# Stick-breaking scan over pairs of columns, with the diagonal cut by a mask matmul

## Chip, core and metric

The kernel runs on one core of one Trainium2 chip. The metric is the time of one execution on the device in microseconds (us), lower is better; a time given for a kernel is the median of several runs.

## What is computed

One decoder layer over 1024 tokens of width 1024, in float32: an input projection, two attention groups side by side (stick-breaking attention with 8 heads of 64, and latent attention with 4 heads), an output projection, and an MLP. The change touches only the stick-breaking group, per head:

```
z = q_blk @ k_pre.T * SB_SCALE
strict = s_idx < t_idx
sp = where(strict, softplus(z), 0)
excl = cumsum(sp, reverse=True) - sp
a = where(strict, exp(log_sigmoid(z) - excl), 0)
out = a @ v_pre
```

Since exp(-softplus(z)) is sigmoid(-z), the weight of column s is sigmoid(z_s) times the product of sigmoid(-z) over the later columns that lie below the diagonal. The kernel computes this product with a running multiplication from the last column to the first.

## The kernel before

The stages of the program are: input projection of the latent columns and of v, then the stick-breaking stage (with the projection of q and k, and later of the latent queries and keys, filled in between its steps), then latent attention, the output projection, and the MLP, whose products take more than half of the time.

The stick-breaking stage has 96 steps. A step is one block of 128 queries of one head (`j` of 0 to 3 in a half `Q` of the sequence) against up to 512 keys (half `C`). Where `C == Q` the block lies on the diagonal and has n = 128, 256, 384 or 512 columns for j = 0 to 3; there are 16 such groups of four. The other 8 groups of four have n = 512 and carry on a product from the diagonal group before them. Of the 96 steps 48 have n = 512.

A step passes over the engines as follows. TensorE (PE) makes the scores `z` with two matmuls. ScalarE (ACT) makes `w = sigmoid(-z)` (L531) and `b = sigmoid(z)` (L532). VectorE (DVE) runs the scan in place over `w`, backwards (L536). The scan's second operand is a slice of `zid`, zeros with an identity at its end: on the diagonal it starts the product at 1 at each row's own diagonal column, and what lies right of it stays 0. The factor `b` is then multiplied by the scan's result, shifted by one column (L542). This multiplication is on GpSimd (POOL) for odd `j`, and for `j` = 2 too in the last three heads; else on DVE. Where a later group needs the product so far, ACT copies one column of `w` into `carry` (L539). Six steps later PE transposes `b` (L549), ACT and DVE split the transposed block into a high part `ah` and a low part `al` (L556, L557), and PE multiplies with v.

PE's instructions stand in the order in which the program is written (a manual schedule). Those of the other engines are put in order by the compiler's scheduler and run in that order, each behind its waits. `w` has three buffers, `b` ten. The first instruction on a new `w` is a memset of its last column on POOL (L529).

The bfloat16 identity `identb` and the mask `mask_incl` for the latent attention are made late, when that stage is prepared; the same kind of mask matmul that the change brings stands at L746 in the latent attention.

Of the kernel before, what the change touches and what calls it, by code (L numbers as in the profile page):

```python
# [9 lines left out]
F32 = mybir.dt.float32  # L10
F32R = mybir.dt.float32r
BF16 = mybir.dt.bfloat16
I32 = mybir.dt.int32
AF = mybir.ActivationFunctionType
ALU = mybir.AluOpType
# [4 lines left out]
NEG = -1e30  # L20
# [3 lines left out]
def tile_hymba_block(  # L24
# [17 lines left out]
    nc = tc.nc  # L42
    P = 128
# [3 lines left out]
    SBH, SBD = 8, 64  # L47
# [13 lines left out]
    const = ctx.enter_context(tc.tile_pool(name="const", bufs=1, reuse_waits="tile"))  # L61
# [2 lines left out]
        nc.vector.memset(f(z_[:, :, 0:P]), 0.0)  # L64
    mhalf = const.tile([P, 16], F32, name="mhalf")
    nc.gpsimd.memset(mhalf[:], -0.5)
    zid = const.tile([P, 4 * P + 1], F32, name="zid")
    nc.gpsimd.memset(zid[:], 0.0)
    identf = zid[:, 3 * P:4 * P]
    make_identity(nc, identf)  # L70
    ones1 = const.tile([P, 1], F32, name="ones1")
    nc.gpsimd.memset(ones1[:], 1.0)
    gc = const.tile([P, gcols.shape[1]], F32, name="gc")
# [442 lines left out]
    sb_a, sb_carry, sb_t, sb_av = {}, {}, {}, {}  # L516

    def sb_z(h, Q, C, j):
        qs, kh, kl = stacks[h]
        diag = C == Q  # L520
        t = 4 * Q + j
        n = (j + 1) * P if diag else 512
        nn = max(n, 256)
        z = z_ps.tile([P, 512], F32, name="z", tag="z")
        ks = slice(C * 512, C * 512 + nn)
        nc.tensor.matmul(z[:, :nn], qs[:, t * P:(t + 1) * P], kh[:, ks], start=True, stop=False)
        nc.tensor.matmul(z[:, :nn], qs[:, t * P:(t + 1) * P], kl[:, ks], start=False, stop=True)
        w = sw_pool.tile([P, 513], F32, name="w", tag="w", bufs=3)
        nc.gpsimd.memset(w[:, n:n + 1], 1.0)  # L529
        b = sw_pool.tile([P, 512], F32, name="b", tag="b", bufs=10)  # L530
        nc.scalar.activation(w[:, :n], z[:, :n], AF.Sigmoid, scale=-SB_SCALE)  # L531
        last_sig[0] = nc.scalar.activation(b[:, :n], z[:, :n], AF.Sigmoid, scale=SB_SCALE)  # L532
        init = 0.0 if diag else sb_carry[h, j][:]
        rv = w[:, :n + 1][:, ::-1]
        inject = zid[:, 4 * P - n:][:, ::-1] if diag else zid[:, 0:1].to_broadcast([P, n + 1])
        nc.vector.tensor_tensor_scan(rv, rv, inject, init, ALU.mult, ALU.add)  # L536
        if C > 0:
            carry = sw_pool.tile([P, 1], F32, name="carry", tag="carry", bufs=4)
            nc.scalar.copy(carry[:], w[:, 0:1])  # L539
            sb_carry[h, j] = carry  # L540
        eng = nc.gpsimd if (j % 2 or (h >= SBH - 3 and j)) else nc.vector
        eng.tensor_mul(b[:, :n], b[:, :n], w[:, 1:n + 1])  # L542
        sb_a[h, Q, C, j] = b

    def sb_tr(h, Q, C, s):
# [52 lines left out]
    def sb_step(n):  # L598
        h = n // 12 + 1
        if n % 12 == 6 and h % 2 and h < SBH - 1:  # L600
            stack_head(h)
        if n == 3 * NS // 4:
            stack_head(SBH - 1, 0)
        if 0 <= n - LAG < NS:
            sb_tr(*idx[n - LAG])
        if n < NS:
            sb_z(*idx[n])
# [5 lines left out]
    fill = in_proj_pair(0)  # L613
# [9 lines left out]
    def in_proj_rest():  # L623
        for p in range(1, NPAIR):
            yield from in_proj_pair(p)
# [18 lines left out]
    fill = in_proj_rest()  # L644
# [35 lines left out]
    def l8(shape, dt=F32R):  # L680
        return lat_pool.tile(shape, dt, name="l8", tag="l8", bufs=5)

    p0_pool = lat.enter_context(tc.tile_pool(name="p0_pool", bufs=1, side="right", reuse_waits="tile"))
    identb = p0_pool.tile([P, P], BF16, name="identb")
    make_identity(nc, identb)
    mask_incl = p0_pool.tile([P, P], BF16, name="mask_incl")
    nc.gpsimd.memset(mask_incl[:], 0.0)
    nc.gpsimd.affine_select(mask_incl[:], mask_incl[:], pattern=[[-1, P]],
                            compare_op=ALU.is_ge, fill=NEG, base=0, channel_multiplier=1)
# [74 lines left out]
    def lat_gen():  # L764
        for h in range(3):
            yield from mla_qk(h, lambda: lat_ps[0]())

    LAT_START = n0 + 3
    fill = lat_gen()
# [151 lines left out]
    s01, n = iter(range(4)), 0  # L921
# [13 lines left out]
    for n in range(n, NTA * (MH - 1)):  # L935
        h, i = divmod(n, NTA)
# [3 lines left out]
        elif 0 < h < MH - 1 and i % 3 < 2:  # L940
            j = i // 3 * 2 + i % 3
# [558 lines left out]
```

## Time and profile before

| | us |
|---|---|
| median of 3 runs | 1235.33 (1234.29 to 1235.84) |
| the profiled execution | 1236.29 |
| its span, first to last instruction | 1234.5 |
| stick-breaking stage in it, first scan to the last steps | 148 to 365, 217 long |
| DVE busy in that stage | 205.5 |
| PE busy in that stage | 180.2 |
| ACT and POOL busy in that stage | 144.3 and 113.7 |

The span is part of the profiled execution's own time; 1.8 us lie around it. Busy time of an engine is the time in which at least one of its instructions ran. An instruction that is held up by another engine after it has started counts as busy, so a duration that is longer than that of its twins is read as a wait.

### The profile page before, as it was taken

The numbers are of one execution on the slowest core, as the hardware profiler recorded it, in microseconds if no ns is written. First come the engines' busy times: TensorE is split into PE (matmuls) and PEld (weight loads), VectorE is DVE, ScalarE is ACT, GpSimd is POOL, SyncE is SP. The second block draws the span as 40 slices with busy tenths as digits, with TensorE's granted clock in tenths as the row PEclk, the third lists the DMA queues.
The fourth block names the chain that finished last, engine by engine and source line by source line (L and its number), as shares of the span: only waits on it lengthen the run. The fifth ranks groups of instructions, "written<-read, shape, count | busy, mean of one in ns | idle before, by whom it ended". The sixth has DMA issues, their size and how long they took to land. (4 is left out here: it accounts for less than half of the span.)

```text
span 1234.5 us, 15926 instructions
## 1 busy us (share of the span) xinstructions
PE 1155.6 (94%) x5424; PEld 941.7 (76%) x5424; DVE 958.0 (78%) x1310; ACT 535.5 (43%) x1080; POOL 647.2 (52%) x539
## 2 busy tenths in 40 slices
PE   9998988888779999999789999999999999999996
PEld 8886866666658888888567788888777888888885
DVE  8686499999997874553979967666498899888995
ACT  6334456667766772245422222222223333333344
POOL 3343454445653353132755655556447766667667
PEclk9999999999999999999889999999999999999998
DMA  6424833332622225475336544443578435454313
GB/s 214 120 68 156 220 82 78 91 91 59 184 107 90 69 69 188 154 255 168 107 130 208 203 151 159 156 154 128 190 248 300 161 119 170 169 171 143 113 52 137
DMA packets 101586, 179.87 MB, mean 146 GB/s; under 512 B 9216, under 2 KB 53760, under 8 KB 100736
## 3 DMA queue, kind: packets, MB, share of 16 engines
q1 hardware_dynamic: 101504, 178.84, 45.0%
q8 instruction: 43, 0.70, 0.2%
q14 instruction: 39, 0.32, 0.1%
HBM read 111.70 MB, written 54.53 MB: 135 GB/s over the span
## 5 line engine op out<-in xcount | busy, mean ns | idle before, releaser
L1437 PE MATMUL dn<-s,s 128*128 128x512 f32 x1344 | 308.6, 392 | 4.4 <-DVE s L1075 2.3
L1437 PEld LDWEIGHTS dn<-s,s 128*128 128x128 f32 x1344 | 254.4, 189 | 58.4 <-DVE s L1075 2.7
L1075 POOL TENSOR_TENSOR s<-ar,s 128x1024 fp32r<-128x1024 f32 x56 | 147.8, 2641 | 80.8 <-ACT s L1074 80.8
L1075 POOL TENSOR_TENSOR s<-s,s 128x512 fp32r<-128x512 f32 x84 | 117.0, 1414 | 109.8 <-ACT s L1074 109.8
L1441 DVE TENSOR_TENSOR acc<-acc,dn 128x512 f32<-128x512 f32 x224 | 144.0, 678 | 33.8 <-PE dn L1437 32.8
L1074 ACT CAST s<-wr 128x1024 fp32r<-128x1024 f32 x48 | 50.4, 1051 | 150.1 <-PE dn L1437 105.3
L1081 PE MATMUL pa<-b,s 128*128 128x512 f32 x384 | 97.2, 407 | 9.0 <-ACT s L1074 3.7
L1081 PEld LDWEIGHTS pa<-b,s 128*128 128x128 f32 x384 | 74.5, 196 | 27.8 <-ACT s L1074 4.6
L1074 ACT CAST s<-s 128x512 fp32r<-128x512 f32 x84 | 48.3, 620 | 103.3 <-DVE s L1199 59.1
L542 POOL TENSOR_TENSOR b<-b,w 128x512 f32<-128x512 f32 (+2 forms) x57 | 59.5, 1044 | 58.9 <-DVE w L536 39.5
L488 PE MATMUL mm<-xh,wt 128*128 128x512 f32 x256 | 87.9, 396 | 0.0
L549 PE MATMUL tr<-zid,b 128*128 128x128 f32 x288 | 52.8, 290 | 36.4 <-DVE al L557 27.3
L549 PEld LDWEIGHTS tr<-zid,b 128*128 128x128 f32 x288 | 32.9, 142 | 60.2 <-DVE al L557 45.2
L1075 POOL TENSOR_TENSOR s<-wr,s 128x1024 fp32r<-128x1024 f32 x24 | 57.8, 2409 | 32.8 <-ACT s L1074 32.8
L263 PE MATMUL acc<-wt,xh 128*128 128x448 f32 (+1 forms) x256 | 64.8, 389 | 0.9 <-ACT xh L214 0.9
L536 DVE TENSOR_TENSOR_SCAN w<-w,zid 128x129 f32<-128x129 f32 (+1 forms) x64 | 63.9, 1001 | 1.0 <-ACT w L531 0.8
L1074 ACT CAST s<-ar 128x1024 fp32r<-128x1024 f32 x56 | 58.6, 1047 | 9.2 <-DMA ar<-hv_dram 9.2
L1075 DVE TENSOR_TENSOR s<-wr,s 128x1024 fp32r<-128x1024 f32 x24 | 52.4, 2182 | 6.8 <-ACT s L1074 6.8
L263 PEld LDWEIGHTS acc<-wt,xh 128*128 128x128 f32 x256 | 49.5, 194 | 8.9 <-ACT xh L214 1.4
L1081 PE MATMUL pb<-t,s 128*128 128x512 f32 x192 | 49.2, 406 | 6.8 <-ACT s L1074 6.7
L488 PEld LDWEIGHTS mm<-xh,wt 128*128 128x128 f32 x256 | 48.1, 189 | 8.3 <-issue 0.2
L1112 DVE SCALAR_TENSOR_TENSOR ho<-ho 128x512 f32<-128x512 f32 x48 | 51.7, 1076 | 1.4
(335 smaller groups left out, 2688.7 us busy)
## 6 DMA issues: line engine op xcount, KB each, us to landing
ar<-hv_dram SPq DMA_DIRECT2D x56, 512.0 KB, 3.6
s<-in_w_up_dram SPq DMA_DIRECT2D x32, 512.0 KB, 4.6
hv_dram<-s SPq DMA_DIRECT2D x64, 256.0 KB, 2.1
wr<-in_w_down_dram SPq DMA_DIRECT2D x16, 1024.0 KB, 6.9
hv_dram<-ho SPq DMA_DIRECT2D x48, 256.0 KB, 2.1
wr<-in_w_in_dram SPq DMA_DIRECT2D x24, 256.0 KB, 2.9
raw<-in_w_o_dram SPq DMA_DIRECT2D x8, 512.0 KB, 3.6
ht<-h_dram SPq DMA_DIRECT2D x8, 512.0 KB, 4.3
```

The source lines that it names most:

```text
L263: nc.tensor.matmul(accs[t][:, :width], a[:, kk, t * P:(t + 1) * P], wts[kk][:, b, :width], start=(kk == 0 and p == 0), stop=done)
L488: nc.tensor.matmul(ps[:], wt[:, a, k % 4, :], b[:, k, tsl], start=(n == 0), stop=(n == 3 * ND - 1))
L536: nc.vector.tensor_tensor_scan(rv, rv, inject, init, ALU.mult, ALU.add)
L542: eng.tensor_mul(b[:, :n], b[:, :n], w[:, 1:n + 1])
L549: nc.tensor.transpose(tr[:, j * P:(j + 1) * P], sb_a[h, Q, C, j][:, s * P:(s + 1) * P], identf[:])
L1074: nc.scalar.copy(hi, src)
L1075: eng.tensor_sub(lo, src, f(hi))
L1081: nc.tensor.matmul(ps, w[:, a, k, :], bv[:, b, k, :], start=start and n == 0, stop=n == last, skip_group_check=True)
L1112: nc.vector.scalar_tensor_tensor(dst, src, 0.0, src, ALU.max, ALU.mult)
L1437: nc.tensor.matmul(ps[:], av[:, a, u, q * P:(q + 1) * P], bv[i][:, b, u], start=i in (1, 2, 7) and n == 0, stop=n == 5, skip_group_check=True)
L1441: read = nc.vector.tensor_add(dst, dst, ps[:])
```

## The change

For each step, neighbouring columns are first multiplied in pairs (even column times odd column, written to the even column of `w`, on DVE), the scan then runs over the n/2 pair products and one last column, and the final multiplication brings each pair's running product to both columns of the pair. What the even column needs beyond that, the factor of its odd neighbour, is multiplied into the even columns of `b` on POOL. So two instructions of n/2 columns with a step of two are added to each step. The diagonal is cut by a third matmul on the scores (bfloat16 identity times a mask with -1e30 on and above the diagonal), so the scan starts with 1 everywhere and its second operand is one zero column, repeated. `carry` is copied by the engine of the final multiplication instead of ACT. That engine is now POOL for odd `j` and DVE for even `j` in all heads. The bfloat16 identity and the new mask are made at the program's start.

```diff
-    zid = const.tile([P, 4 * P + 1], F32, name="zid")
+    zid = const.tile([P, P + 1], F32, name="zid")
     nc.gpsimd.memset(zid[:], 0.0)
-    identf = zid[:, 3 * P:4 * P]
+    identf = zid[:, 0:P]
     make_identity(nc, identf)
+    zero1 = zid[:, P:P + 1]
+    identb = const.tile([P, P], BF16, name="identb")
+    nc.vector.tensor_copy(identb[:], identf)
+    mask_strict = const.tile([P, P], BF16, name="mask_strict")
+    nc.gpsimd.memset(mask_strict[:], 0.0)
+    nc.gpsimd.affine_select(mask_strict[:], mask_strict[:], pattern=[[-1, P]],
+                            compare_op=ALU.is_gt, fill=NEG, base=0, channel_multiplier=1)
...
-        nc.tensor.matmul(z[:, :nn], qs[:, t * P:(t + 1) * P], kl[:, ks], start=False, stop=True)
+        nc.tensor.matmul(z[:, :nn], qs[:, t * P:(t + 1) * P], kl[:, ks], start=False, stop=not diag)
+        if diag:
+            nc.tensor.matmul(z[:, n - P:n], identb[:], mask_strict[:], start=False, stop=True)
...
-        init = 0.0 if diag else sb_carry[h, j][:]
-        rv = w[:, :n + 1][:, ::-1]
-        inject = zid[:, 4 * P - n:][:, ::-1] if diag else zid[:, 0:1].to_broadcast([P, n + 1])
-        nc.vector.tensor_tensor_scan(rv, rv, inject, init, ALU.mult, ALU.add)
+        init = 1.0 if diag else sb_carry[h, j][:]
+        even, odd = w[:, 0:n:2], w[:, 1:n:2]
+        nc.vector.tensor_mul(even, even, odd)
+        nc.gpsimd.tensor_mul(b[:, 0:n:2], b[:, 0:n:2], odd)
+        rv = w[:, 0:n + 1:2][:, ::-1]
+        nc.vector.tensor_tensor_scan(rv, rv, zero1.to_broadcast([P, n // 2 + 1]), init, ALU.mult, ALU.add)
+        eng = nc.gpsimd if j % 2 else nc.vector
         if C > 0:
             carry = sw_pool.tile([P, 1], F32, name="carry", tag="carry", bufs=4)
-            nc.scalar.copy(carry[:], w[:, 0:1])
+            eng.tensor_copy(carry[:], w[:, 0:1])
             sb_carry[h, j] = carry
-        eng = nc.gpsimd if (j % 2 or (h >= SBH - 3 and j)) else nc.vector
-        eng.tensor_mul(b[:, :n], b[:, :n], w[:, 1:n + 1])
+        b2 = b[:, :n].rearrange("p (k a) -> p k a", a=2)
+        eng.tensor_mul(b2, b2, w[:, 2:n + 1:2].unsqueeze(2).to_broadcast([P, n // 2, 2]))
```

How the instructions stand is shown for the start of one diagonal group in the middle of the stage. The first two pieces are DVE's. A scan has the name SCALAR_TENSOR_TENSOR here and TENSOR_TENSOR_SCAN in the profile; L536 is the scan, L542 the final multiplication, L557 the split of a transposed block. DVE before, a group's four steps (j = 0 to 3):

```order
L536 SCALAR_TENSOR_TENSOR w<-w,zid 128x129
L542 TENSOR_TENSOR b<-b,w 128x128
L152 TENSOR_TENSOR zpad_59<-tr,zpad_59 128x128
L473 CAST wt<-wr 128x512
L536 SCALAR_TENSOR_TENSOR w<-w,zid 128x257
L557 TENSOR_TENSOR al<-tr,ah 128x512
L536 SCALAR_TENSOR_TENSOR w<-w,zid 128x385
L542 TENSOR_TENSOR b<-b,w 128x384
```

DVE of the change at the same place, where L544 is the multiplication of neighbours, L547 the scan, L554 the final multiplication, L569 the split and L480 the cast:

```order
L544 TENSOR_TENSOR w<-w 128x64
L159 TENSOR_TENSOR zpad_59<-tr,zpad_59 128x128
L547 SCALAR_TENSOR_TENSOR w<-w,zid 128x65
L544 TENSOR_TENSOR w<-w 128x128
L554 TENSOR_TENSOR b<-b,w 128x128
L547 SCALAR_TENSOR_TENSOR w<-w,zid 128x129
L480 CAST wt<-wr 128x512
L569 TENSOR_TENSOR al<-tr,ah 128x512
L544 TENSOR_TENSOR w<-w 128x192
L547 SCALAR_TENSOR_TENSOR w<-w,zid 128x193
L554 TENSOR_TENSOR b<-b,w 128x384
```

Each scan now has a multiplication ahead of it, often directly, that writes what the scan reads. Over the stage 28 scans were followed directly by the multiplication that reads their result; now 84 DVE instructions (60 scans, 13 final multiplications, 11 copies of `carry`) stand directly behind the one whose result they read.

The second place is POOL's queue there. POOL before, from the final multiplication (L542) of the last step of the group ahead; L529 is the memset of `w`'s last column (L474 and L495 are the low parts of a weight block and of a projected block):

```order
L542 TENSOR_TENSOR b<-b,w 128x512
L529 MEMSET w 128x1 x2
L542 TENSOR_TENSOR b<-b,w 128x256
L529 MEMSET w 128x1
L474 TENSOR_TENSOR wt<-wr,wt 128x512
L495 TENSOR_TENSOR klo<-y,khi 128x512
```

POOL of the change at the same place, where L545 is the multiplication of the even columns of `b`, L554 the final multiplication, L538 the memset, and L481 and L502 the low parts:

```order
L554 TENSOR_TENSOR b<-b,w 128x512
L545 TENSOR_TENSOR b<-b,w 128x64
L538 MEMSET w 128x1 x2
L545 TENSOR_TENSOR b<-b,w 128x128
L554 TENSOR_TENSOR b<-b,w 128x256
L538 MEMSET w 128x1
L481 TENSOR_TENSOR wt<-wr,wt 128x512
L502 TENSOR_TENSOR klo<-y,khi 128x512
L545 TENSOR_TENSOR b<-b,w 128x192
```

POOL has one more multiplication in every step. The one for j = 2 (128x192) stands behind two 128x512 subtractions, and DVE's final multiplication for j = 2 (L554, 128x384) reads its result.

## Rows read from the trace of the kernel before

**Rows 1.** Page, busy time of the engines, share of the span, instructions.

```profile
PE 1155.6 (94%) x5424; PEld 941.7 (76%) x5424; DVE 958.0 (78%) x1310; ACT 535.5 (43%) x1080; POOL 647.2 (52%) x539
```

**Rows 2.** Stage 148 to 365 us: all instructions, those of L536, those of L542.

```profile
148.00:365.00 217.00, 180.17 (x926) 138.97 (x924) 205.54 (x269) 144.28 (x360) 113.66 (x184) 0.99 0.39 101
...
148.00:365.00 217.00, 112.71 (x96) 0.99 0.39 101
...
148.00:365.00 217.00, 30.61 (x39) 59.23 (x57) 0.99 0.39 101
```

**Rows 3.** Waits in the stage: who waited for whom, us, times, longest.

```profile
POOL b L542 <- DVE w L536: 39.5, 30, 1.7
...
ACT carry L539 <- DVE w L536: 32.4, 29, 3.5
...
PE tr L549 <- DVE al L557: 26.1, 34, 2.2
...
DVE al L557 <- ACT ah L556: 4.9, 9, 0.7
```

**Rows 4.** Timeline of DVE and POOL: start us, us, engine, line, instruction.

```profile
240.85 1.28 POOL L474 TENSOR_TENSOR wt<-wr,wt 128x512 fp32r<-128x512 f32 x1
...
241.24 1.44 DVE L536 TENSOR_TENSOR_SCAN w<-w,zid 128x257 f32<-128x257 f32 x1
...
242.09 1.68 POOL L495 TENSOR_TENSOR klo<-y,khi 128x512 fp32r<-128x512 f32 x1
...
249.22 1.41 POOL L587 TENSOR_TENSOR ssq_s<-ssq_s,avt 64x512 f32<-64x512 f32 x1 [0.76 <-ACT avt L586]
...
249.66 1.53 DVE L542 TENSOR_TENSOR b<-b,w 128x512 f32<-128x512 f32 x1
```

**Rows 5.** Timeline of DVE at moments without a longer twin's delay.

```profile
319.74 0.44 DVE L536 TENSOR_TENSOR_SCAN w<-w,zid 128x129 f32<-128x129 f32 x1
320.28 0.29 DVE L542 TENSOR_TENSOR b<-b,w 128x128 f32<-128x128 f32 x1
320.49 0.68 DVE L557 TENSOR_TENSOR al<-tr,ah 128x512 fp32r<-128x512 f32 x1
...
329.92 0.68 DVE L536 TENSOR_TENSOR_SCAN w<-w,zid 128x257 f32<-128x257 f32 x1
...
331.95 0.95 DVE L536 TENSOR_TENSOR_SCAN w<-w,zid 128x385 f32<-128x385 f32 x1
...
236.87 1.21 DVE L536 TENSOR_TENSOR_SCAN w<-w,zid 128x513 f32<-128x513 f32 x1
...
216.02 0.56 DVE L542 TENSOR_TENSOR b<-b,w 128x384 f32<-128x384 f32 x1
...
227.20 0.69 DVE L542 TENSOR_TENSOR b<-b,w 128x512 f32<-128x512 f32 x1
```

**Rows 6.** Single lines over the whole trace: minimum/median/maximum ns, shapes.

```profile
L536 DVE TENSOR_TENSOR_SCAN w<-w,zid x64: 395/1002/2008, 148.0 to 352.8; 128x129 f32<-128x129 f32 x16, 128x257 f32<-128x257 f32 x16, 128x385 f32<-128x385 f32 x16, 128x513 f32<-128x513 f32 x16
L536 DVE TENSOR_TENSOR_SCAN w<-w,carry,zid x32: 1270/1286/2328, 161.8 to 362.7; 128x513 f32<-128x513 f32 x32
...
L542 POOL TENSOR_TENSOR b<-b,w x57: 637/1093/2012, 150.9 to 364.2; 128x512 f32<-128x512 f32 x35, 128x256 f32<-128x256 f32 x16, 128x384 f32<-128x384 f32 x6
L542 DVE TENSOR_TENSOR b<-b,w x39: 273/692/1533, 148.5 to 357.5; 128x128 f32<-128x128 f32 x16, 128x512 f32<-128x512 f32 x13, 128x384 f32<-128x384 f32 x10
...
L557 DVE TENSOR_TENSOR al<-tr,ah x80: 404/658/694, 156.3 to 371.2; 128x512 fp32r<-128x512 f32 x48, 128x384 fp32r<-128x384 f32 x16, 128x256 fp32r<-128x256 f32 x16
...
L529 POOL MEMSET w<- x96: 93/99/265, 131.6 to 358.3; 128x1 f32 x96
...
L746 PEld LDWEIGHTS <-identb x32: 95/96/98, 363.9 to 462.3; 128*128 128x128 bf16 x32
L746 PE MATMUL s<-mask_incl,identb x29: 229/230/232, 375.6 to 462.3; 128*128 128x128 bf16 x29
```

**Rows 7.** Groups by line and shape, DVE: busy us, mean ns.

```profile
L757 DVE RECIPROCAL mst<-mst 128x1 f32<-128x1 f32 x32 | 5.1, 159 | 8.7 <-ACT pt L756 8.5
```

More of the change, by code (lines that the diff above doesn't have):

```diff
@@ L683, in tile_hymba_block @@
     p0_pool = lat.enter_context(tc.tile_pool(name="p0_pool", bufs=1, side="right", reuse_waits="tile"))
-    identb = p0_pool.tile([P, P], BF16, name="identb")
-    make_identity(nc, identb)
     mask_incl = p0_pool.tile([P, P], BF16, name="mask_incl")
```

## The prediction, made before the changed kernel was run

> **What bounds the kernel now.** The page gives PE 94% of the span and DVE 78% [rows 1], which would make a change on DVE worth nothing. That average hides the stage. The scans run from 148 to 365 us, and there DVE is busy 205.5 of 217 us, PE 180.2, ACT 144.3, POOL 113.7 [rows 2]. DVE is idle for 11.5 us, PE for 37, and the waits say what PE lacks: the largest share of its matmul waits there ends with DVE's low part `al` [rows 3]. DVE in turn waits little for anyone (4.9 us for ACT's `ah`). POOL (39.5 us) and ACT (32.4 us, at the copy of `carry`) wait for DVE's scan [rows 3]. So DVE sets the length of this stage, and outside it the change does next to nothing.
>
> The second thing to see is in DVE's durations. The same scan of 257 columns takes 0.68 us at one time and 1.44 at another [rows 4, 5]. The long one began at 241.24 while POOL's subtraction ran until 242.13, and ended 0.55 later, at 242.68; POOL's next one, begun at 242.09, took 1.68 and ended 1.09 after the scan. The multiplication of 512 columns that takes 0.69 alone began at 249.66, sat out POOL's 1.41 until 250.63, and ended at 251.19 [rows 4, 5]. A DVE instruction with both inputs in SBUF and a POOL one that reads SBUF thus run one after the other. The low part `al`, whose first input lies in PSUM, has a maximum of 0.694 for 512 columns, so it is not held up [rows 6]. Part of DVE's 205.5 us is therefore waiting for POOL.
>
> How much: the 48 shorter-than-512 scans and the 16 diagonal ones of 513 take 16 x (0.44 + 0.68 + 0.95 + 1.21) = 52.5 alone, the 32 with a carry 32 x 1.286 = 41.2 [rows 5, 6], together 93.6; they were busy 112.7 [rows 2], 19.1 more. DVE's 39 final multiplications take 16 x 0.29 + 10 x 0.56 + 13 x 0.69 = 19.2 alone and were busy 30.6, 11.4 more [rows 2, 5, 6]. That is 30.5 us over 135 instructions, 0.23 us each.
>
> **The change on DVE's own work.** Scans: (1.21 - 0.44) / 384 = 2.0 ns per column [rows 5]. With 65, 129, 193 and 257 columns they take 0.31, 0.44, 0.57 and 0.68 alone, with a carry 0.07 more (1.286 against 1.21). New sum 16 x 2.00 + 32 x 0.75 = 56.0, so 37.6 are saved. Added are 96 multiplications of neighbours, n/2 columns each. At the rate of the final multiplication, (0.69 - 0.29) / 384 = 1.04 ns per column [rows 5], they take 0.22, 0.29, 0.36 and 0.42: 16 x 1.29 + 32 x 0.42 = 34.0. Nine final multiplications come over from POOL (6 x 0.56 + 3 x 0.69 = 5.4), and 16 copies of `carry` from ACT; the nearest DVE row of one column is 0.16 [rows 7], 2.6 in all. Sum: -37.6 + 34.0 + 5.4 + 2.6 = **+4.4**.
>
> Instructions also overlap or gap. One that doesn't need its neighbour starts 0.08 before that ends (0.29 from 320.28, next at 320.49); one that reads what its neighbour wrote starts 0.10 after (0.44 from 319.74, next at 320.28) [rows 5]. The order has 28 such direct pairs before and 84 after: 56 x 0.18 = +10.1. The 122 additional instructions give back 122 x 0.08 = 9.8. So +0.3, and DVE's own work grows by about **5 us**: halving the scan buys nothing, since the pair products cost what it saves.
>
> **The unknown stride.** No row shows a DVE instruction that steps over every second float. Below, the step is free. Above, it costs as much as the slowest rate per column here, the scan's 2.0 ns: 0.96 more on 16 x (64 + 128 + 192) + 48 x 256 = 18,432 columns, +17.8, and on the final multiplication's 16 x (128 + 384 + 512) = 16,384, +15.8. The scan takes 2 ns per column already and I give it nothing. I take free: the multiplication by a contiguous neighbour is the nearest row in kind, and two of every four floats that lie together are still read.
>
> [...]
>
> **Waiting for POOL.** POOL gains 96 multiplications. Its own take 0.637 at 256 and 1.093 at 512 columns [rows 6], so 1.8 ns per column and 0.30, 0.41, 0.52, 0.64 for 64 to 256: 16 x 1.87 + 32 x 0.64 = 50.4. Its final ones shrink from 35 x 1.09 + 16 x 0.64 + 6 x 0.87 (between the two) = 53.6 to 32 x 1.09 + 16 x 0.64 = 45.1. The rest of its reading work is 113.7 - 59.2 - 96 x 0.1 = 44.9 [rows 2, 6]. So POOL's time with a read goes from 98.5 to 140.4, by 1.43. DVE's exposed instructions go from 135 to 96 + 96 + 48 = 240. If the wait follows POOL's time it becomes 30.5 x 1.43 = 43.6 (+13); if each instruction still waits 0.23, it is 54.2 (+24). Both are possible, since the added POOL pieces are short; I take the middle, **+18**.
>
> **Other waits.** DVE's final multiplication for j = 0 and 2 now needs POOL's product on `b`, which stands behind POOL's other work, in the piece shown behind two subtractions of 1.3 us. POOL has 140 + 10 us of work in some 240, so it usually gets there; with a full subtraction's wait at the 18 or so places where low parts are made this could reach +23. Against that ACT no longer stands at `carry` for 32.4 us, so `ah` comes sooner, at most the 4.9 us that DVE waits for it [rows 3]. I take **+3**.
>
> PE gains 64 mask matmuls of 0.23 and weight loads of 0.10 [rows 6]. At most 15 us, and its 37 idle us hide them; were the stage bound by PE they would all count. ACT loses 32 copies. Making the mask early is work of under a microsecond on POOL, done while the first loads are under way.
>
> **Sum.** 5 + 18 + 3 = 26 us on the profiled execution's 1236.3 gives 1262. The median of the runs shown is 1.0 below that execution, so **1261 us**, the stage 243 instead of 217.
>
> **Rivals.**
> - The step costs on DVE. Then 17.8 for the pair products, or 33.6 with the final multiplication, come on top: 1279 to 1295. POOL would also be held up longer. Nothing in the trace speaks for or against it.
> - POOL's queue becomes the limit, because its product of two floats per repeated factor runs slower than the contiguous one, or because DVE waits for the even products at each low part: up to +23 - 3, so 1281. For it: two reads in every POOL step that were none. Against it: 150 us of work in a stage of 243 leave POOL time to catch up.
> - Faster: the waits at the SBUF input shrink instead of growing. Scans of half the length hold it for half as long, POOL gets through between them, and its shorter pieces hold DVE for less. With 5 us of own work more and 3 of other waits, the balance is at 30.5 - 8 = 22.5 us over 240 instructions, 0.09 us each in place of 0.23. At 0.04 (10 us) the stage would take 204 and the kernel 1223. Against it: POOL's reading time grows by 42 us in a stage in which DVE already fills 95%.
> - No change: ACT's freed queue and half of that effect just pay for the rest, 1235.
>
> **Chances and range.** Forecast (1245 to 1275) 0.50; stride 0.20; POOL's queue 0.13; faster 0.12; no change 0.05. Slower by over 0.2%, about what a measurement of this kernel can tell from no change: 0.83; within it 0.05; faster 0.12. The range leaves out the faster case and part of no change, and the far end of the stride: 1240 to 1297. The forecast's own range is 1245 to 1275.
>
> **What would show it.** In the stage: scans of 257 columns at 0.68 to 0.75 alone (right on the scan), pair products of 256 at 0.42 (free step) or nearer 0.7 (it costs), pairs directly behind each other 0.10 apart. The sum of excess on DVE's exposed instructions near 48 us (right on the input), under 22 (the faster rival), over 60 (worse). DVE busy over 90% of a longer stage, with PE idle for more than 37 us. Wrong would be a DVE with long idle times that end with POOL's `b`, or a stage in which PE is busy throughout. Outside 148 to 400 us all should stand as before, moved by a constant.

## The result and the profile after

The changed kernel took 1262.95 us (median of four runs, 1261.25 to 1263.32) against 1235.45 for the kernel before on the same chip: a ratio of 1.0221, with a 95% interval of 1.0204 to 1.0239. It is slower by 27.5 us. The forecast was 1261, in a range of 1240 to 1297.

The loss lies in the stick-breaking stage. Its first scan still starts at 147 to 148 us, its last ends at 390.5 instead of 364.0, and what stands before and after has only moved. The page's first part, which answers to [rows 1], shows little of it:

```profile
PE 1165.2 (92%) x5488; PEld 947.5 (75%) x5488; DVE 987.1 (78%) x1432; ACT 534.9 (42%) x1048; POOL 701.1 (56%) x642
```

The windows of the stage answer to [rows 2]. The columns are the window and its length, busy time and instructions of PE, PE's weight loads, DVE, ACT and POOL, the granted clock (as a share of full speed), the DMA share and GB/s. The first row is everything. Then come the scan (L547, DVE alone), the final multiplication (L554, DVE then POOL), the pair product (L544, DVE) and the product on `b` (L545, POOL).

```profile
147.00:391.00 244.00, 191.34 (x992) 144.73 (x990) 235.65 (x390) 144.26 (x328) 166.64 (x285) 0.97 0.35 90
...
147.00:391.00 244.00, 79.11 (x96) 0.97 0.35 90
...
147.00:391.00 244.00, 36.98 (x48) 44.44 (x48) 0.97 0.35 90
...
147.00:391.00 244.00, 60.62 (x96) 0.97 0.35 90
...
147.00:391.00 244.00, 71.98 (x96) 0.97 0.35 90
```

DVE's scans went from 112.7 to 79.1 us, waits included, and the new pair products took 60.6. DVE is busy for 235.7 of 244 us, 30.1 more than before, and idle for 8.3 (before 11.5). PE is idle for 53. POOL went from 113.7 to 166.6 us.

How much of DVE's time is work and how much is being held up is read by setting instructions that nothing held up beside longer ones of the same shape. The timeline of DVE and POOL in the changed kernel (start, duration, engine, line, instruction; in brackets the idle time ahead and what ended it) has both kinds:

```profile
207.90 0.34 DVE L547 TENSOR_TENSOR_SCAN w<-w,zid 128x65 f32<-128x65 f32 x1
208.35 0.29 DVE L554 TENSOR_TENSOR b<-b,w 128x128 f32<-128x128 f32 x1
...
208.76 0.28 DVE L544 TENSOR_TENSOR w<-w 128x128 f32<-128x128 f32 x1
209.07 0.64 DVE L547 TENSOR_TENSOR_SCAN w<-w,zid 128x129 f32<-128x129 f32 x1
...
229.91 0.42 DVE L544 TENSOR_TENSOR w<-w 128x256 f32<-128x256 f32 x1
...
230.85 0.75 DVE L547 TENSOR_TENSOR_SCAN w<-w,carry,zid 128x257 f32<-128x257 f32 x1
...
246.35 0.86 POOL L545 TENSOR_TENSOR b<-b,w 128x256 f32<-128x256 f32 x1
...
246.75 0.74 DVE L544 TENSOR_TENSOR w<-w 128x256 f32<-128x256 f32 x1
...
248.37 1.09 POOL L554 TENSOR_TENSOR b<-b,w 128x512 f32<-128x512 f32 x1 [1.15 <-DVE w L547]
```

The pair product of 256 columns takes 0.42 us alone (229.91). The one at 246.75 began while POOL's product on `b` ran until 247.21, and ended at 247.49, 0.28 later. The new POOL instruction thus holds up the new DVE instruction, in the way that [rows 4] showed for the old ones. This holds for the whole stage: of its 240 scans, pair products and final multiplications on DVE, 121 ran more than 0.08 us over the shortest durations of their shape, and each of the 121 began while a POOL instruction that reads SBUF was running. For 62 of them, with 24 of the 63 us of excess, it was the new product; for 31, with 16 us, a final multiplication. Ninety began with no such instruction running, and none of them was that long; of the other 29, 25 began in the last 0.2 us of one. The whole trace gives minimum, median and maximum ns of each line:

```profile
L547 DVE TENSOR_TENSOR_SCAN w<-w,carry,zid x32: 735/758/1764, 164.6 to 389.8; 128x257 f32<-128x257 f32 x32
...
L544 DVE TENSOR_TENSOR w<-w x96: 193/550/1500, 147.4 to 388.6; 128x256 f32<-128x256 f32 x48, 128x64 f32<-128x64 f32 x16, 128x128 f32<-128x128 f32 x16, 128x192 f32<-128x192 f32 x16
...
L545 POOL TENSOR_TENSOR b<-b,w x96: 343/842/1231, 146.8 to 386.0; 128x256 f32<-128x256 f32 x48, 128x64 f32<-128x64 f32 x16, 128x128 f32<-128x128 f32 x16, 128x192 f32<-128x192 f32 x16
```

The waits of the stage, which answer to [rows 3], name DVE once more as the engine that PE lacks, and show DVE hardly waiting for POOL's product on a semaphore (columns as there):

```profile
PE tr L561 <- DVE al L569: 37.3, 31, 2.7
POOL b L554 <- DVE w L547: 27.2, 28, 3.6
...
DVE b L554 <- POOL b L545: 3.0, 4, 1.8
```

### The profile page after: what moved, and what is told of

The parts are those of the page before. It is cut to its first block, busy times and chain, and to the rows that moved or that the text cites. A ratio compares the mean times of both kernels' runs of the same rounds, so it can differ in the third digit from the quotient of the medians.

```text
span 1261.4 us, 16273 instructions
## 1 busy us (share of the span) xinstructions
PE 1165.2 (92%) x5488; PEld 947.5 (75%) x5488; DVE 987.1 (78%) x1432; ACT 534.9 (42%) x1048; POOL 701.1 (56%) x642
## 5 line engine op out<-in xcount | busy, mean ns | idle before, releaser
L495 PE MATMUL mm<-xh,wt 128*128 128x512 f32 x256 | 92.0, 411 | 0.0
L545 POOL TENSOR_TENSOR b<-b,w 128x64 f32<-128x64 f32 (+2 forms) x96 | 72.2, 755 | 3.4 <-ACT b L541 3.0
L554 POOL TENSOR_TENSOR b<-b,w 128x512 f32<-128x512 f32 (+1 forms) x48 | 45.2, 941 | 29.0 <-DVE w L547 27.2
L568 ACT CAST ah<-tr 128x512 fp32r<-128x512 f32 (+2 forms) x80 | 42.0, 525 | 44.7 <-PE tr L561 44.4
L544 DVE TENSOR_TENSOR w<-w 128x64 f32<-128x64 f32 (+2 forms) x96 | 60.6, 631 | 0.1
```

The costliest lines, as they stand in the source:

```text
L495: nc.tensor.matmul(ps[:], wt[:, a, k % 4, :], b[:, k, tsl], start=(n == 0), stop=(n == 3 * ND - 1))
L544: nc.vector.tensor_mul(even, even, odd)
L545: nc.gpsimd.tensor_mul(b[:, 0:n:2], b[:, 0:n:2], odd)
L554: eng.tensor_mul(b2, b2, w[:, 2:n + 1:2].unsqueeze(2).to_broadcast([P, n // 2, 2]))
L568: nc.scalar.copy(ah[:, lo:], tr[:, lo:])
```

## Experiments

The theory was that of the prediction. Work: the pair products cost DVE what the halved scan saves. Input: POOL's new product costs the rest, by holding DVE at the SBUF input. Its rivals were POOL's queue (DVE waiting for the product's result), PE's new matmuls, the moved copies and multiplications, and the step of two. Each kernel was timed beside the kernel before, whose median was then 1234.5 to 1235.1 us. The diffs are against the changed kernel, or against the kernel before where it says so.

### The mask alone

The kernel before with the diagonal cut by the mask matmul, a scan that starts at 1 and one repeated zero column:

```diff
+        if diag:
+            nc.tensor.matmul(z[:, n - P:n], identb[:], mask_strict[:], start=False, stop=True)
...
-        inject = zid[:, 4 * P - n:][:, ::-1] if diag else zid[:, 0:1].to_broadcast([P, n + 1])
+        inject = zid[:, P:P + 1].to_broadcast([P, n + 1])
```

> The kernel before with the mask matmul alone: 64 mask matmuls on PE, the scan at full length and started at 1, its second operand a repeated zero. Theory (DVE's work and the SBUF input it shares with POOL set the stage): PE's idle time hides the matmuls, DVE's work is the same, so 1233 to 1239 us. Rival (the mask matmuls and a lower PE clock in the stage make the loss): 64 times 0.23 to 0.33 us more, 1250 us or above.

1234.37 us, 0.9995 [0.9985, 1.0005]. PE's 64 added matmuls are hidden: in the stage PE was busy for 186.0 of the same 217 us. This part of the change costs nothing.

### Without POOL's product, without DVE's product, without either

The first of the three leaves out POOL's product on `b`:

```diff
-        nc.gpsimd.tensor_mul(b[:, 0:n:2], b[:, 0:n:2], odd)
```

> The changed kernel without POOL's multiplication of the even columns of b (the factor of the odd neighbour is left out of the result). Theory: DVE's own work stays, POOL reads SBUF some 66 us less, so the excess on DVE's exposed instructions falls from about 64 to about 35 us; 1230 to 1242 us. Rival (DVE's own added instructions make the loss, POOL doesn't matter): 1257 us or above.

1237.16 us, 1.0016 [1.0007, 1.0026]. Without POOL's product the change is worth +2.6 us. That is not DVE's own work alone. In this run's stage DVE's excess over undisturbed durations is 40 us, some 9 more than before, and about as much comes back from closer neighbours and less idling. So halved scan and pair products come out nearly even on DVE, but the +2.6 is a sum and does not measure the prediction's +4.4 by itself.

The second leaves out the pair product:

```diff
-        nc.vector.tensor_mul(even, even, odd)
```

> The changed kernel without DVE's multiplication of neighbours (the scan runs over the even columns alone, so the running product lacks the odd ones). Theory: DVE loses 33 us of work, up to 28 us of waiting in it and some gaps; PE with 190 us of work takes over as the limit, so the stage falls from 244 to 190 to 205 us and the kernel to 1208 to 1224 us. Rival (the length of DVE's queue doesn't set the stage): 1245 us or above.

1241.69 us, 1.0049 [1.0034, 1.0064], far above what was expected and below the rival's 1245. The waits and the window of its stage say why:

```profile
DVE b L553 <- POOL b L544: 32.5, 34, 2.8
```

```profile
148.00:370.00 222.00, 189.01 (x986) 145.39 (x985) 183.50 (x293) 143.69 (x328) 168.42 (x283) 0.95 0.38 98
```

DVE is now idle for 39 of 222 us, 32.5 of them for POOL's product. With DVE's queue shorter, POOL's becomes the limit. The prediction's rival on the queue was wrong for the change and right just behind it, so taking out the pair product can't price the pair product.

The third leaves out both:

```diff
-        nc.vector.tensor_mul(even, even, odd)
-        nc.gpsimd.tensor_mul(b[:, 0:n:2], b[:, 0:n:2], odd)
```

> The changed kernel without either added multiplication (scan over the even columns alone, even columns of b not multiplied; the result lacks both factors). Theory, as corrected by the run without DVE's product, in which DVE waited 32 us for POOL's product: with both gone neither DVE nor POOL is the limit, PE with 190 us of work is, and the kernel takes 1205 to 1222 us. Rival (something else in the change, such as the moved final multiplications or the mask, keeps the stage long): 1235 us or above.

1198.59 us, 0.9711 [0.9692, 0.9729], 6 us under the lower end of what was expected. The four kernels make a table:

| | no product on POOL | product on POOL |
|---|---|---|
| no pair product on DVE | 1198.6 | 1241.7 |
| pair product on DVE | 1237.2 | 1263.0 |

With neither product, the halved scan and the rest of the change (mask, copies, moved multiplications) gain 36 us. The window of that kernel's stage shows what stops it there:

```profile
144.00:326.00 182.00, 175.22 (x991) 140.94 (x990) 171.62 (x293) 143.23 (x328) 99.11 (x189) 1.00 0.47 120
```

PE is busy for 175 of 182 us, so PE sets this stage as much as DVE does. The pair product takes 38.6 us back, and POOL's product costs 43.1 alone or 25.8 on top of the other. Together they cost 64.4, less than 38.6 + 43.1. That each hides part of the other's wait is the likely reading, not a shown one.

### POOL's product added to the kernel before

Against the kernel before (the second factor is `b`'s own odd columns, so that nothing new waits for `w`):

```diff
+        nc.gpsimd.tensor_mul(b[:, 0:n:2], b[:, 0:n:2], b[:, 1:n:2])
```

> The kernel before with one more POOL multiplication in each step, of n/2 columns of b with a step of two, that waits for b alone (the result is changed by it). DVE's instructions are those of before. Theory: the excess on DVE's 135 exposed instructions grows from 30 us to 45 to 60, so 1247 to 1262 us. Rival (POOL's added work is hidden): 1234 to 1240 us.

1258.64 us, 1.0189 [1.0174, 1.0204], in the range expected. The path was only partly the one foreseen:

```profile
146.00:387.00 241.00, 186.29 (x929) 143.71 (x927) 211.25 (x268) 145.98 (x360) 188.97 (x279) 0.96 0.35 91
```

```profile
DVE b L543 <- POOL b L541: 18.2, 24, 1.8
```

DVE's busy time grew by 5.7 us only, to 211.3 of 241, and it is idle for 30, of which 18.2 end with POOL's product. So 96 products on POOL cost 24 us in the old kernel and 26 in the new one, but in the old one chiefly as a queue, in the new one as longer DVE instructions. An estimate, mostly from undisturbed durations, fits this. DVE's instructions with two inputs in SBUF and POOL's reading ones take 112.8 + 98.5 = 211 us in the old stage of 217. With the 96 products of this run, 48.5 us at their shortest durations (0.61 us at 256 columns), they come to 260 in a stage of 241.

### The step of two on POOL

POOL's product on columns that lie together (and a wrong column as factor):

```diff
-        nc.gpsimd.tensor_mul(b[:, 0:n:2], b[:, 0:n:2], odd)
+        nc.gpsimd.tensor_mul(b[:, 0:n // 2], b[:, 0:n // 2], w[:, n // 2:n])
```

> The changed kernel with POOL's added multiplication on n/2 columns that lie together, b[0:n/2] times w[n/2:n], in place of every second one (the result is changed by it, and it waits for the pair product, since w's right half is written by it). Theory: the step of two is what makes this multiplication take 0.85 us at 256 columns where 0.64 was foreseen; lying together it takes 0.64 again, some 16 us less of POOL's reading, and the kernel takes 1252 to 1260 us. Rival (the step costs nothing, the duration comes from something else): 0.85 us stays.

1286.71 us, 1.0421 [1.0405, 1.0437], a miss. The edit brought a wait of its own: the factor now lies in columns that the scan overwrites, so the scan waits for POOL.

```profile
DVE w L547 <- POOL b L545: 48.4, 66, 3.0
```

Its time says nothing of the step. Its durations do: undisturbed products of 256 columns took 0.72 to 0.74 us, against 0.86 with the step in the change and 0.61 with the step in the kernel above, where both factors are columns of `b`. A contiguous final multiplication of 256 takes 0.64 [rows 6]. Between the first two the step would explain 0.13 of the 0.22 us beyond that, but the 0.61 with a step of two speaks against a price of the step as such; see Open, below.

### The moved copy and the moved multiplications

```diff
-            eng.tensor_copy(carry[:], w[:, 0:1])
+            nc.scalar.copy(carry[:], w[:, 0:1])
```

> The changed kernel with carry copied by ACT again. Theory: ACT isn't the limit and the copies are short, so 1258 to 1265 us, at most 2.4 us of DVE's copies less. Rival (freeing ACT's queue is worth what ACT waited at the copy): 1270 us or above.

1267.37 us, 1.026 [1.0242, 1.0277], between the two expectations. With the copy back on ACT, ACT stood at it for 42.1 us and DVE's idle time in the stage doubled to 16.4 us.

```profile
ACT carry L551 <- DVE w L547: 42.1, 30, 5.1
```

Taking the copy off ACT was worth some 4 us to the change; beside the halved scan it is the one part that gained.

```diff
-        eng = nc.gpsimd if j % 2 else nc.vector
+        eng = nc.gpsimd if (j % 2 or (h >= SBH - 3 and j)) else nc.vector
```

> The changed kernel with the final multiplication for j = 2 of the last three heads back on POOL, as before. Theory: DVE loses 9 multiplications of 0.56 or 0.69 us and their waits of about 0.26, some 8 us, POOL gains 9 of 0.87 or 1.09, of which a part comes back as waits; 1255 to 1262 us. Rival (POOL's queue is what counts by now): 1264 us or above.

1261.31 us, 1.0217 [1.0201, 1.0233], within the expected range but not to be told from the change. The nine multiplications that came over to DVE, and the three copies of `carry` that go with them, cost nothing that shows.

### The scan's input moved to PSUM

If the hold-up at the SBUF input is real, a scan with only one input in SBUF should lose it. Against the kernel before, ACT writes sigmoid(-z) over `z` in PSUM, the scan reads it there, and `w` takes the result, its last column set by POOL. The two sigmoids change places with it:

```diff
-        nc.scalar.activation(w[:, :n], z[:, :n], AF.Sigmoid, scale=-SB_SCALE)
-        last_sig[0] = nc.scalar.activation(b[:, :n], z[:, :n], AF.Sigmoid, scale=SB_SCALE)
+        nc.scalar.activation(b[:, :n], z[:, :n], AF.Sigmoid, scale=SB_SCALE)
+        last_sig[0] = nc.scalar.activation(z[:, :n], z[:, :n], AF.Sigmoid, scale=-SB_SCALE)
...
-        nc.vector.tensor_tensor_scan(rv, rv, inject, init, ALU.mult, ALU.add)
+        nc.vector.tensor_tensor_scan(rv, z[:, :n][:, ::-1], inject, init, ALU.mult, ALU.add)
```

> The kernel before with sigmoid(-z) written back over the scores in PSUM, so that the scan's first input lies in PSUM and one input alone in SBUF; the last column of w is set apart (0 on the diagonal, else a copy of carry). Same result. Theory (a DVE instruction is held up by POOL only with both inputs in SBUF): no scan over its own duration, the excess of 20 us on the scans is gone and POOL's multiplications are not held by them; 1212 to 1228 us, unless the score banks, held until the scan's end, stop PE. Rival (the long scans are long for another reason, such as memory traffic): their spread of 0.4 to 2.3 us stays, 1233 us or above.

1214.01 us, 0.9831 [0.9817, 0.9846], faster than both kernels. Minimum, median and maximum of the scans, and the window of the stage:

```profile
L539 DVE TENSOR_TENSOR_SCAN w<-z,zid x64: 396/816/1224, 146.5 to 332.7; 128x128 f32<-128x128 f32 x16, 128x256 f32<-128x256 f32 x16, 128x384 f32<-128x384 f32 x16, 128x512 f32<-128x512 f32 x16
L539 DVE TENSOR_TENSOR_SCAN w<-z,carry,zid x32: 1267/1273/1283, 159.9 to 341.9; 128x512 f32<-128x512 f32 x32
```

```profile
146.00:343.00 197.00, 178.31 (x925) 141.01 (x925) 181.92 (x267) 147.36 (x359) 103.90 (x183) 1.00 0.43 111
```

No scan was held up: the longest took 1.22 and 1.28 us, where the old ones reached 2.01 and 2.33 [rows 6]. In the same run DVE's final multiplications, which still have both inputs in SBUF, reached 1.54 us, as before:

```profile
L545 DVE TENSOR_TENSOR b<-b,w x39: 278/680/1539, 146.9 to 337.3; 128x128 f32<-128x128 f32 x16, 128x512 f32<-128x512 f32 x13, 128x384 f32<-128x384 f32 x10
```

The scan's work is as long as before (92.7 us in the stage, against the 93.6 undisturbed of the kernel before); DVE's busy time fell from 205.5 to 181.9 us and POOL's from 113.7 to 103.9.

PE now waits for the scan to release `z` (44.7 us, matmuls and weight loads together). A third buffer for `z`, at the price of one of the two that collect the output, was to give that back:

```diff
-    z_ps = sb_pool("z_ps", 2, space=PSUM)
+    z_ps = sb_pool("z_ps", 3, space=PSUM)
...
-    av_ps = sb_pool("av_ps", 2, space=PSUM)
+    av_ps = sb_pool("av_ps", 1, space=PSUM)
```

> The scan from PSUM with three banks for the scores and one in place of two for the sums of weights times v. Theory: in the run with two banks PE waited 45 us for a scan to give its bank back, and DVE was idle 15 us; with a third bank DVE sets the stage alone, 1203 to 1212 us. Rival (the single bank for the sums stops PE 16 times): 1213 us or above.

1230.98 us, 0.9967 [0.9955, 0.9978], a miss: 17 us slower than with two and two. PE stops at the only output buffer.

```profile
PE av L572 <- DVE ob L580: 28.4, 14, 3.6
...
PEld av L572 <- DVE ob L580: 23.6, 11, 4.1
```

The last kernel keeps the scan from PSUM, adds the change's mask matmul, and takes the weight as the difference of two neighbouring running products. This makes the second sigmoid unnecessary (the diff is against the kernel before, and leaves out what the mask run and the scan from PSUM show above):

```diff
-        last_sig[0] = nc.scalar.activation(b[:, :n], z[:, :n], AF.Sigmoid, scale=SB_SCALE)
...
-        eng.tensor_mul(b[:, :n], b[:, :n], w[:, 1:n + 1])
+        eng.tensor_sub(b[:, :n], w[:, 1:n + 1], w[:, :n])
```

> The scan from PSUM, with the mask matmul, and the weight formed as the difference of neighbouring running products (excl times sigmoid(z) equals excl minus excl times sigmoid(-z)), so ACT's second sigmoid is gone; two score banks as before. Theory: DVE's instructions are the same, so its 182 us are the floor; the score bank is free 0.6 us sooner in each step, so PE waits less, and the kernel takes 1200 to 1214 us. Rival (POOL's subtraction of 1.28 us at 512 columns in place of 1.09, or its queue, takes that back): 1215 us or above.

1211.01 us, 0.9807 [0.9786, 0.9828], the lowest time of those that compute all of the layer. ACT's busy time in the stage fell to 111.3 us, but DVE's hardly (180.7 of 194), so only 3 us came of it, and this interval overlaps that of the scan from PSUM.

## Why the prediction was right

The time was 2 us from the forecast, and the mechanism was the one forecast: DVE's own work stays nearly the same, and waiting at the SBUF input grows. That it came within 2 us is luck in part, because several terms were off and cancelled. With the measured waits for POOL and the other terms as predicted, the forecast would have been 1276. In the stage:

| term of the sum | predicted | measured |
|---|---|---|
| DVE's own work | +4.4 | +2.4 |
| how neighbours overlap or gap (measured: the rest of DVE's busy time) | +0.3 | -5.7 |
| waiting for POOL | +18 | +33.4 |
| other waits (DVE idle) | +3 | -3.1 |
| sum | +26 | +27 |

**DVE's own work: right.** Undisturbed, scans of 65 to 257 columns take 0.28, 0.43, 0.56, 0.68 and with a carry 0.75, pair products 0.20, 0.28, 0.34, 0.42, final multiplications 0.28, 0.55, 0.69, the copy 0.15 (the 0.56 of 193 columns is from the run without POOL's product; here the shortest was 0.62). So 16 x 1.95 + 32 x 0.75 + 16 x 0.82 + 48 x 0.42 + 16 x 1.52 + 16 x 0.15 = 115.2 us, against 93.6 + 19.2 = 112.8 before.

**The step of two on DVE: free, as taken.** From 128 to 256 columns a pair product grows by (0.42 - 0.28) / 128 = 1.09 ns per column, near the contiguous 1.04, and final multiplications take what they took before. So this rival falls.

**Waiting for POOL: the right place, the wrong size.** The excess over undisturbed durations is 79.1 - 55.2 = 23.9 us on scans, 60.6 - 33.3 = 27.3 on pair products and 37.0 - 24.3 = 12.7 on final multiplications: 63.9 over 240 instructions, 0.27 each, where 30.5 over 135, 0.23 each, stood before. By the prediction's own signs that is over 60, on the side of "worse". The term was mis-sized at two points. The middle was taken between "follows POOL's time" (43.6) and "each instruction waits as long as before" (54.2); the second was nearer, and the measured excess lies above both. And POOL's product took 0.86 us at 256 columns, not 0.64. It was busy for 72.0 us and not 50.4; at undisturbed durations it would have been 66. The faster rival needed 0.09 each and had its sign wrong: shorter instructions were not held for less.

That the scans are held up by way of their second input in SBUF is shown by the scan that reads PSUM: it took 1.28 us at most, where the one with both inputs in SBUF took up to 2.33 [rows 6]. The hold-up is not confined to two inputs, though. In the changed kernel the cast of a weight block, with one input in SBUF, takes 0.40 us undisturbed, but 1.52 where it began behind a POOL subtraction that ran until 218.42; it ended at 218.70, 0.28 later:

```profile
217.13 1.29 POOL L502 TENSOR_TENSOR qlo<-y,qhi 128x512 fp32r<-128x512 f32 x1
217.18 1.52 DVE L480 CAST wt<-wr 128x512 fp32r<-128x512 f32 x1
```

The stage has only seven such casts, 4.6 us in all against 4.1 before, so they don't change the sum.

**Neighbours: the gap was too wide.** The 0.10 us came from a scan and the multiplication behind it, and those still have it (207.90 + 0.34 to 208.35). The new pairs are mostly the other way round, product then scan, and there the gap is 0.03 (208.76 + 0.28 to 209.07), as it is from scan to copy. By an estimate, the 60 scans and 11 copies that stand directly behind what they read give back 71 x 0.07 = 5 us of the 6 by which this term was off. The -5.7 is what is left of DVE's busy time, so it holds whatever else changed on DVE too.

**Other waits: the sign was wrong.** DVE waited only 3.0 us for POOL's product, and the freed ACT, put at no more than 4.9, was worth some 4 when the copy was put back. The queue rival needed a DVE that runs ahead of POOL; that came where the pair product was taken out (32.5 us of waiting) and where the old kernel got POOL's product (18.2). It and the mask's zero cost are settled by runs.

**Open.** Why POOL's product took 0.86 us in the change, 0.73 with its columns together and 0.61 with the step inside one tile was not settled. DVE is not the reason: in the run without the pair product seven of them stood wholly in DVE's idle time and took 0.83 to 0.87 us, and the 0.73 and 0.61 occur beside an idle DVE too. Nor is it the step alone: the subtraction of the last kernel, contiguous and within one tile, also takes 0.61 at its 256 columns (the shortest in the row, 607 ns):

```profile
L552 POOL TENSOR_TENSOR b<-w x57: 607/1036/1037, 149.4 to 341.0; 128x512 f32<-128x512 f32 x35, 128x256 f32<-128x256 f32 x16, 128x384 f32<-128x384 f32 x6
```

By these rows the long duration comes with a step of two and a second tile together; what makes it is open.

## What to carry to other kernels

Halving a long instruction by putting another ahead of it saves nothing if the added one costs about the same on the same engine, so count both, fixed parts included (here, undisturbed, the scans fell by 38.4 us and the pair products added 33.3). Where VectorE instructions with both inputs in SBUF are held up by GpSimd's reads, as here (a pair product of 256 columns took 0.42 us undisturbed and 0.74 behind GpSimd's product), add GpSimd's reading time to VectorE's before giving GpSimd more to do, even if it looks half idle; in this kernel 96 small products on it cost 24 to 43 us, depending on what else stood in the queues. The better lever was to move one input to PSUM, which took 21 us off without any less arithmetic; but then ask who waits for that buffer (here TensorE, 44.7 us).

## What was not expected of the hardware

- A step of two floats cost DVE next to nothing (1.09 ns per column against 1.04 contiguous; 0.42 us for a pair product of 256 columns), while POOL's products of 256 columns ran at 0.86, 0.73 and 0.61 us depending on step and tiles.
- The time from one DVE instruction to the next that reads its result depends on the pair: 0.11 us from scan to multiplication, 0.03 from multiplication to scan or from scan to copy.
- The same POOL instruction cost 43 us in the kernel without pair products on DVE, and 26 in the one with them.
- DVE's cast with one input in SBUF was held up too (0.40 us undisturbed, 1.52 behind a POOL subtraction).
